# Thresholded attention on one core: first queries loaded and transposed another way, the last two groups' queries picked by one-hot products, and a new step order

## The chip, the cores and the metric

The kernel runs on one core of a Trainium2 chip. A core has five engines with an instruction queue each: TensorE (PE in the profile; its weight loads are PEld), VectorE (DVE), ScalarE (ACT), GpSimd (POOL) and SyncE (SP), which here only issues DMAs. The metric is the device time of one execution in microseconds, the median of several runs.

## What is computed

Eight batches of twelve heads, 512 queries and keys of 64 numbers. Softmax weights at or under the threshold are set to zero, and the rest is normalised again:

```python
batch, heads, seq, dim = 8, 12, 512, 64          # Q, K, V float32, threshold 0.1
scores = np.einsum('bhqd,bhkd->bhqk', Q, K) * scale
weights = np.exp(scores - np.max(scores, axis=-1, keepdims=True))
weights = weights / (np.sum(weights, axis=-1, keepdims=True) + 1e-10)
weights = np.where(weights > threshold, weights, 0)
weights = weights / (np.sum(weights, axis=-1, keepdims=True) + 1e-10)
return np.einsum('bhqk,bhkd->bhqd', weights, V)
```

With random inputs few weights pass the threshold, and most output rows are zero.

## The kernel before

**Cheap pass, over everything.** The 96 heads are 48 pairs (`hp`, two heads each), 24 quads (`hq`) and 12 groups (`j`, eight heads). For every pair the keys and queries are brought to a layout with the 64 numbers on the partitions. Keys: loaded as float32, transposed on PE (`ktr`, line 336), evicted from PSUM (`kev`, to `kt`, float32), cast to float16 by POOL (`kf`). Queries: loaded by quads in runs of 1 KB (`load_q`), cast to float16 (`qmix`, POOL or VectorE), transposed (`qtr`, line 369), evicted (`qev`). Then for each of four chunks of 128 keys one PE step makes the transposed scores of both heads (`qk`, line 379), 128 x 1024 in PSUM, and ACT takes the exponential (`exp`, line 385) or VectorE approximates it through the bits of an integer (line 387): 192 such steps. Products with a matrix `groups` (`d`, line 391; eight steps of four products for a pair) and a maximum (`dred`, line 399) tell for every query whether it may have a weight above the threshold.

**Exact pass, over the rows found.** Once for each group, 32 slots for each of its four pairs: `flags`, `size` (a bound on the norms, from `qsq` and `ksq`), `rank` (a running count on PE), `key`; `oh` compares slot numbers with the ranks and gives one-hot columns (line 428); `idx` multiplies them with row numbers (line 439); `half` and `idxev` make the index; `gather` fetches the found query rows by an indirect DMA of POOL; `split` puts each into the half of its head; `xtr` transposes them (line 467), `xev` evicts; `xqk` makes their exact scores in float32 (line 479); `xexp`, `tv`, `found` (line 496), `vidx`; `fetch` gets the value rows by an indirect DMA into a zeroed tile (`vzero`); `scatter` writes them to the output, which `z` (512 KB zero writes, on SP) has cleared. The names `load_first_q`, `do_first_tr` and `do_first_ev` are the first quad's own path: its queries are loaded as float32 pairs in runs of 256 bytes, half of them by ACT's queue, and transposed as float32 on PE (line 348). `heat`, `warm` and `spare` are products of zeros on PE without a user.

**Order.** Every step is declared with `add(name, {engine: (occupation, latency)}, dependencies, ...)`. The table `ORDER` holds a finished result of a search: the steps in program order, two digits each, and a string of bits that says which engine takes a step that has a choice. Each engine runs its own steps strictly in that order, and waits where a dependency isn't ready. PSUM is three tiles `sc` (128 x 1024) and two tiles `sm` (128 x 512); key loads have six buffers of a pair, query loads four of a quad. In program order the end of the kernel is: last exponentials, `dred` 46 and 47, `flags` to `idxev` of group 11, and the gather, split, products, fetch and scatter of groups 9, 10 and 11.

Of the kernel before, what the change touches and what calls it, by code (L numbers as in the profile page):

```python
# [55 lines left out]
def kernel(  # L56
# [19 lines left out]
    nc = tc.nc  # L76
# [39 lines left out]
    def by_pairs(ap):  # L116
# [16 lines left out]
        "0401020005060D0BN7N0080t0703N2N5N3090L0J0P0A0M0C0K0u0Q0E0NN4N10F0v200G0H0cN60x210s0O0y0z0d0-0g0a0+0R0S0T120U0V1K"  # L133
        "0W100e0X0Y0h0b22110Z240f15261628190i0j0k1A252p3y2n2o0l170m1R270r2B130n0o29181S2A1P141L1N1B1Q1C1D1E1M2T1F0p1G0q2W"
        "2E1H1I1O1T1U1c2s1J2u1d1V1W2X2F1X2r2C1Y1Z2D1a2t2a2I2w1b1e1f2b2v2y1g2J2x2G2U1h1i2-1j2V2H312Y2K301k3x3w4j4i4h1l3-3E"
        "412L332M2N1m2O322Z1n1o2m341p2P2z3H2+2Q2R432S3I443+3F40423G454m35362c3738393A2d3B3C3J4l3K3L4n2e3D3M2f4p2g462h2i2j"
        "6d2l4C48473N4o3O3P5q3Q3R4A2k3S3T4D493U3V4N4s4q4O4U4B4E4F4G4H4I4r581q1r4J4K4L4P4V3X3W1s3Y1y4S4v5s4M6b5r5v4T1t1u3Z"
        "5x5D4Q4w5E5u3a5z4g4R5+5Q4t4u5w5y3b3c4W3d4X4Y5B4Z4z3e4x3f5C5-4+3g8X6c7m4a4b604y6H1v4c3h4d3i4e5F594-50615152536454"
        "5A5G5566625H5I5J5K4f6Z1w6563675L565M5N5O6f9g3j6K6L6g575P6i6h6k68696A6B6C6D6M6I6j5S6E6m6l5R6F5T5U6G6N6J3k5V5W5X3l"
        "6O721x3m5Y6P796n7A5Z6o7l7k8W8VAR233n7p5a7r3o6r6t6p6s5b7K5c6u7t6Q6R6q7o7q7s73771z5d7v7u7L74786S6v6w6T6U6V6x756y6W"  # L140
        "6X6z6+6-7w808T6Y769f4k7x707B710w7C7y7D7E818B8a8c3p5e7F7+7G7H7I7z8e8C7J8Z7-8f8G8b5f8283848D858d6a5g3q8U9e7nAPAQ8H"
        "86875h1+889j7M8g9l898I5i8A8J8E8l7N8F7O9n8y5t7P8j8m8k9o8h8z8i8K7Q8L5j7R9i8-8+7S9k7T8n8MBZBa0ICL909m8N7U938O8P8Q8R"
        "9EAT8oBY7V7W8SAN9F9p9194AV9w8p928q8rAX8s8t8u8v9u8w95967XAU9798999v9A9x9BA5AW9CAC9s8x9q9DAYADAa9G9H9I9tAZ9JA8A69r"
        "5k9KA99y9z9+9L9M7YAsA79-AxAfA05mAg7ZB9AA7aBd5lA1Ay7bA2ABA37cAbAc7gAhAv9NA4AEAiAFAGAH9OAIAdAwBcAtAeBeCJCKDU3zBf9P"
        "9QAuBhAJAzAKBgALCNCPA+Bi9RAOCO7dAMBjCRBmBkBlDTCQB-A-B0B1B2B3B4B5BqAjAkB6AlAmBoAnFOBnAoBrApBpB7CHAqCSArC0C6C2BsC1"
        "BtCTDSEDEFC3CUBA9SCmDXBuDZC7BvBwBxBy9TBz9UB+CVCXCY9VCWCZDWB8D2CpDY9WBBBCCaDaBDC4BECqBFCnCbCIBGDbC5C8CcBHDcEBD33r"
        "9a1-CoDdC9CACBCCEI3sDv9XEKCtDgCdG9FMEECDCECeCfCFCgChDeCuDhCGDfDiBICiCjCkCrBJEHDjBKCsClDkEJEMCvCwELENCxCyCzC+9YC-"
        "D0DlD1BLE0DwEOD4ETDmEgDnE1D5DoD6DxFREUDpD77eD8EREnEjDqESEoEkFNHI6e7fFTBMDrDsD9DtDADuEVEPBND+FVBOEWEzEQDBFWBPD-Dy"
        "FQEhEiFSBQEXEYEZEaG7EbDCDzElGBEcG5DDBRECDEEdFU7h5n3tEeEfG8BSGCGDFXGEFcEm2qGFEpEqGGFYFaHHHGI3FdFpFZErEsGHEtE2E3Eu"
        "FeE4EvEw5o7iFbFfE5E6FqE7E8ExE9FgDFGIBUFrI1JCDVI2FsFwFtFhFiFjFkFlFmEyEAFxGaBTE+FnE-GJHLFuHNFoF0FvF1HPF2GNHKGKHQDG"  # L150
        "GbHMDHGOGtF3DIGPHOGcF4GsF5DJGQFyGfGLFzF+DKF-G0G1G2BV5pHRHjF6GhJAJBJzCMGgG6GMGdHUF7F8GiI6G3GRGSHVG4GTGUGVGeGWHkGX"
        "GYHYHSGjGkHlHTGlGmGZ7jF9DLGnGoGpDMI8GqIAHZI5GrIBGuHoJFJH9ZI7HmGvJJI4HpHnHWGwI9GxGyGzI0H-JKICHqIDHXG+HrIFIEHaHbIU"
        "FAIGJvG-HcHdFBHeHfHgIXJE3uFC9bDNIVJGIYJIHhFDJLIJIWIHHiIZFEIIH0HsHtJdHuIKHvIaHwH1HxBbHyHzJwH2IbJMJiILH+IMINIO9hJD"
        "L6J+JxJyL5IcIPIQJNIRJjK03vFFH3K2ISJQJgJRIdIeIfIgIhIiIjIkJ-ImInLrITJOIlJhIoK1JSIpK4JPIqK3JkJeIrL48YLtJTK5K6JUJlIs"
        "KOJVItJWJXIuJfKPFG9cK9KBJmJnJoJYJZJpJqJaJbKQKCL9H4FILBJrJsLwJtFHKAK7K8L8KVLAJcJuKWLDH5H6LsHJGAL7FPFJLCLEKDKEKTKR"
        "H7KUKFLFLXLyKGLILvKSASLGLxH8LJLHLzKHDOH99dM0MIDPKIKJKKKLKgKhLpKMKXKYKZLKHALMKNLLLNKaKbL+KcLYLZLaLeL-LOLPKdLQKeLR"
# [53 lines left out]
    def load_first_q(hp, other=nc.sync):  # L210
        q_sb = kload.tile([P, R, 2, D], f32, name="k_sb")
        for part in load_pair(q_sb, Qp, hp, other):
            keep(part)
# [550 lines left out]
```

## Time and profile before

| | us |
|---|---|
| median of 3 runs (lowest, highest) | 208.61 (207.15, 209.53) |
| the profiled execution | 208.51 |
| its span, first to last instruction | 206.8 |
| PE, VectorE, ACT, POOL busy in the span | 183.9, 171.0, 163.1, 108.8 |
| first exponential starts | 7.68 |
| last exponential ends | 181.07 |
| last `flags` starts | 185.11 |
| last scatter's instruction ends | 202.55 |

The mean granted TensorE clock was 0.969 of full speed. PE's times are modelled at their ends, so a busy PE isn't PE at its peak. In lines of the profile a row begins with the line of the kernel, the engine and the operation, then output and inputs by name; in lines in order of time it begins with start and duration in us, and what stands in brackets is the engine's idle time before it and what ended that. DMAs moved 38.86 MB in 69,589 packets, 54,356 of them under 512 bytes.

### The profile page before, as it was taken

The numbers are of one execution on the slowest core, as the hardware profiler recorded it, in microseconds if no ns is written. First come the engines' busy times: TensorE is split into PE (matmuls) and PEld (weight loads), VectorE is DVE, ScalarE is ACT, GpSimd is POOL, SyncE is SP. The second block draws the span as 40 slices with busy tenths as digits, with TensorE's granted clock in tenths as the row PEclk, the third lists the DMA queues.
The fourth block names the chain that finished last, engine by engine and source line by source line (L and its number), as shares of the span: only waits on it lengthen the run. The fifth ranks groups of instructions, "written<-read, shape, count | busy, mean of one in ns | idle before, by whom it ended". The sixth has DMA issues, their size and how long they took to land.

```text
span 206.8 us, 7766 instructions
## 1 busy us (share of the span) xinstructions
PE 183.9 (89%) x3235; PEld 122.4 (59%) x3237; DVE 171.0 (83%) x320; ACT 163.1 (79%) x194; POOL 108.8 (53%) x176
## 2 busy tenths in 40 slices
PE   7888999999999999999999988899989999868900
PEld 4554758666756677576677566576657567652200
DVE  6679998999889899989999795989979989642650
ACT  2798998979989999998999988879978899601200
POOL 5025046607467419254656776286665666344661
PEclk9999999999999999999999999999999999696995
DMA  6999799783996599749776279999399500000000
GB/s 138 238 288 258 185 257 269 212 224 89 277 338 190 182 284 275 206 109 251 231 236 149 75 204 241 384 394 210 101 323 412 220 6 8 10 8 4 7 13 11
DMA packets 69589, 38.86 MB, mean 188 GB/s; under 512 B 54356, under 2 KB 66276, under 8 KB 69552
## 3 DMA queue, kind: packets, MB, share of 16 engines
q1 hardware_dynamic: 67344, 37.50, 64.4%
q0 software_dynamic: 1152, 0.59, 1.7%
q8 instruction: 26, 0.43, 0.9%
q10 hardware_dynamic: 1056, 0.26, 0.6%
q14 instruction: 11, 0.09, 0.2%
HBM read 25.95 MB, written 12.98 MB: 188 GB/s over the span
## 4 chain that ended last, share of the span: by engine, by line
PE 65%; DVE 13%; issue 6%; ACT 5%; DMA 4%; POOL 3%; another core or an unknown queue 1%; POOLq 1%; SPq 0%; DVEq 0%; ACTq 0%
PE sc L379 22%; PE sm L391 19%; DVE e L387 6%; PE sc L336 5%; PE sm L479 4%; PE sm L412 4%; PE sm L369 3%; ACT e L385 3%; PE sm L439 3%; DMA k_sb<-in_K_dram 2%; DVE stat L399 2%; DVE qt L321 2%; DMA vsel<-in_V_dram,vidx 1%; PE sc L259 1%; POOL out_dram L193 1%
## 5 line engine op out<-in xcount | busy, mean ns | idle before, releaser
L385 ACT ACTIVATE e<-sc 128x1024 bf16<-128x1024 f32 x140 | 135.8, 1031 | 13.0 <-PE sc L379 11.8
L379 PE MATMUL sc<-qt,kf 64*128 64x512 f16 x384 | 65.2, 384 | 4.5 <-DVE e L387 2.8
L391 PEld LDWEIGHTS <-e 128*128 128x128 bf16 x1536 | 52.5, 99 | 24.4 <-issue 23.8
L387 DVE TENSOR_SCALAR e<-sc 128x1024 int16<-128x1024 f32 x52 | 63.2, 1218 | 4.5 <-PE sc L379 3.2
L391 PE MATMUL sm<-groups,e 128*128 128x64 bf16 x1536 | 62.8, 194 | 2.0 <-issue 1.2
L323 POOL CAST kf<-kt 128x512 f16<-128x512 f32 x46 | 29.7, 660 | 45.1 <-ACT kt L319 34.2
L399 DVE TENSOR_REDUCE stat<-sm 128x8 f32<-128x512 f32 x48 | 32.6, 684 | 9.6 <-PE sm L391 3.0
L379 PEld LDWEIGHTS <-kf 64*128 64x128 f16 x384 | 18.9, 94 | 19.5 <-issue 11.2
L323 POOL CAST qm<-q_sb 128x512 f16<-128x512 f32 x40 | 26.9, 684 | 3.2 <-DMA q_sb<-in_Q_dram 3.1
L193 POOL DMA_INDIRECT qsel<-in_Q_dram,idx x12 | 13.3, 1108 | 18.7 <-DVE idx L448 13.7
L336 PE MATMUL sc<-identity_f,k_sb 64*128 64x64 f32 x368 | 19.3, 226 | 0.7 <-DMA k_sb<-in_K_dram 0.7
L336 PEld LDWEIGHTS sc<-identity_f,k_sb 64*128 64x128 f32 x368 | 16.7, 138 | 3.7 <-DMA k_sb<-in_K_dram 1.0
L319 ACT COPY kt<-sc 128x1024 f32<-128x1024 f32 x16 | 16.2, 1013 | 1.4 <-PE sc L379 0.7
L193 POOL DMA_INDIRECT vsel<-in_V_dram,vidx x12 | 12.9, 1076 | 3.3 <-issue 1.6
L321 DVE COPY qt<-sm 128x1024 f16<-128x1024 f16 x20 | 13.6, 682 | 1.2 <-PE sc L379 1.2
L369 PE MATMUL sm<-identity_h,qm 128*128 128x128 f16 x184 | 14.1, 219 | 0.5 <-DVE stat L399 0.5
L193 POOL DMA_INDIRECT out_dram<-vsel,idx x12 | 12.8, 1064 | 3.2 <-issue 2.9
L479 PE MATMUL sm<-kt,xq 128*32 128x512 f32 x96 | 13.7, 642 | 0.9 <-DVE xq L321 0.6
L359 DVE TENSOR_SCALAR qsq<-qt 128x1024 int16<-128x1024 int16 x24 | 13.3, 560 | 0.0
L369 PEld LDWEIGHTS <-qm 128*128 128x128 f16 x184 | 10.6, 97 | 2.6 <-issue 2.2
L412 PE MATMUL sm<-heads,qsq 128*128 128x2 bf16 x192 | 11.0, 163 | 1.0 <-issue 1.0
L412 PE MATMUL sm<-heads,ksq 128*128 128x2 bf16 x192 | 11.4, 165 | 0.5 <-issue 0.5
(94 smaller groups left out, 168.5 us busy)
## 6 DMA issues: line engine op xcount, KB each, us to landing
out_dram<-zero SPq DMA_DIRECT2D x24, 512.0 KB
k_sb<-in_K_dram SPq DMA_DIRECT2D x95, 128.0 KB
q_sb<-in_Q_dram SPq DMA_DIRECT2D x23, 512.0 KB
k_sb<-in_Q_dram SPq DMA_DIRECT2D x3, 128.0 KB
qsel<-in_Q_dram,idx POOLq DMA_INDIRECT x12, 4.5
vsel<-in_V_dram,vidx POOLq DMA_INDIRECT x12, 3.0
out_dram<-vsel,idx POOLq DMA_INDIRECT x12, 2.2
k_sb<-in_K_dram ACTq DMA_DIRECT2D x1, 128.0 KB
```

What stands on the lines that cost most here:

```text
L193: return keep(nc.gpsimd.indirect_dma_start(**args))
L321: keep(nc.vector.tensor_copy(dst, src))
L323: keep(nc.gpsimd.tensor_copy(dst, src))
L336: keep(nc.tensor.matmul(buffer("sc", ("ktr", hq))[:, at:at + D], lhsT=k_sb[rows, r, :, :].rearrange("p h d -> p (h d)"), rhs=identity_f32[ ...
L369: keep(nc.tensor.matmul(buffer("sm", ("qtr", hq))[:].bitcast(f16)[:, at], lhsT=buffer("qm", hq)[:, at], rhs=identity_h[:], is_transpose=Tr ...
L379: keep(nc.tensor.matmul(buffer("sc", ("qk", hp, c))[:, h * S:(h + 1) * S], lhsT=pair("kf", hq)[ps, n, c * P:(c + 1) * P], rhs=pair("qt", h ...
L385: keep(nc.scalar.activation(e[:], sc[:], ACTF.Exp, scale=scale))
L387: keep(nc.vector.tensor_scalar(e[:].bitcast(i16), sc[:], BITS_A, BITS_B, op0=ALU.mult, op1=ALU.add))
L391: keep(nc.tensor.matmul(buffer("sm", ("d", hp))[:, j * G:(j + 1) * G], lhsT=buffer("e", (hp, c))[:, j * P:(j + 1) * P], rhs=groups[:], sta ...
L399: keep(nc.vector.tensor_reduce(T["stat", j][:, n, :], buffer("sm", ("d", hp))[:].rearrange("p (c g) -> p c g", g=G), axis=AX.X, op=ALU.max))
L412: keep(nc.tensor.matmul(rk[:, at:at + 2], lhsT=sq[:, n % 2, r * P:(r + 1) * P], rhs=heads[:], start=True, stop=True))
L479: keep(nc.tensor.matmul(buffer("sm", ("xs", j))[sl, :], lhsT=xq[:, sl], rhs=pair("kt", 2 * j + n // 2)[:, n % 2], start=True, stop=True, t ...
```

## The change

Four things. The first quad's queries come like all others: quad layout, runs of 1 KB, cast to float16 by `qmix`, and transposed as float16; their first half is one DMA on ACT's queue, ahead of all others. Both halves of the first keys go out on SP. For the last two groups (10 and 11) the one-hot is float32 in another layout, `idx` uses a float32 copy of the row numbers, and a new step `sel` multiplies the queries, which still lie in SBUF, with the one-hot, straight into the layout that `xev` evicts; `gather`, `split` and `xtr` are gone for these groups. `ORDER` is a new search result, with its declared durations changed in places.

```diff
-    load_k(0, nc.scalar)
+    q_sb = qload.tile([P, 4, R, D], f32)
+    T["q", 0] = q_sb
+
+    def load_first_q(n, eng):
+        keep(eng.dma_start(out=q_sb[:, 2 * n:2 * n + 2].rearrange("p h r d -> p h (r d)"), in_=Q4[0][:, 2 * n:2 * n + 2]))
+
     load_first_q(0, nc.scalar)
+    load_k(0)
+    load_first_q(1, nc.sync)
     load_k(1)
-    load_first_q(1)
...
+        keep(nc.vector.tensor_copy(row_f[:], row_no[:]))
...
     def do_first_tr(n, which, eng):
-        tp = buffer(("sm", "sc")[which], ("first", n))
-        src = T.pop((("k", "q32")[which], n))
         for r in range(R):
-            keep(nc.tensor.matmul(tp[:, r * P:(r + 1) * P], lhsT=src[:, r, :, :].rearrange("p h d -> p (h d)"),
-                                  rhs=identity_f32[:], is_transpose=True, start=True, stop=True))
+            at = slice(r * P, (r + 1) * P)
+            if which == 0:
+                keep(nc.tensor.matmul(buffer("sm", ("first", n))[:, at], lhsT=T["k", n][:, r, :, :].rearrange("p h d -> p (h d)"),
+                                      rhs=identity_f32[:], is_transpose=True, start=True, stop=True))
+            else:
+                keep(nc.tensor.matmul(buffer("sc", ("first", n))[:].bitcast(f16)[:, at], lhsT=pair("qm", 0)[:, n, at],
+                                      rhs=identity_h[:], is_transpose=True, start=True, stop=True))
...
     def do_onehot(j, eng):
...
+        if j >= NO - 2:
+            oh = work.tile([P, C2, 4, SLOTS], f32, name="oh_f")
+            keep(nc.vector.tensor_tensor(
+                out=oh[:], in0=slot_no[:, :, 0].unsqueeze(1).unsqueeze(1).to_broadcast([P, C2, 4, SLOTS]),
+                in1=key.rearrange("p n c -> p c n").unsqueeze(3).to_broadcast([P, C2, 4, SLOTS]), op=ALU.is_equal))
...
     def do_idx(j, eng):
...
+            if j >= NO - 2:
+                one, rows = oh.rearrange("p c n s -> p c (n s)")[:, c, :], row_f
...
+    def do_sel(j, eng):
+        oh = T["oh", j]
+        for n in range(4):
+            q_sb = T["q", 2 * j + n // 2]
+            for r in range(R):
+                for h in range(2):
+                    keep(nc.tensor.matmul(buffer("sm", ("xp", j))[h * D:(h + 1) * D, n * SLOTS:(n + 1) * SLOTS],
+                                          lhsT=q_sb[:, 2 * (n % 2) + h, r, :], rhs=oh[:, h * R + r, n, :],
+                                          start=(r == 0), stop=(r == R - 1), tile_position=(0, h * D)))
...
+        if near:
+            stage("sel", {"PE": (0.95, 1.2)}, [("oh", j)] + [("q", hq) for hq in (2 * j, 2 * j + 1)], do_sel, takes=[("sm", ("xp", j))], gives=[("oh", j)])
+        else:
+            stage("gather", {"POOL": (1.45, 6.4, 0.1)}, [("idxev", j)] + ([("split", j - NS)] if j >= NS else []), do_gather)
+            stage("split", {"POOL": (0.4, 0.55), "DVE": (0.21, 0.37)}, [("gather", j), ("half", j)], do_split, takes=[("qb", j)])
+            stage("xtr", {"PE": (0.17, 0.40)}, [("split", j)], do_xtr, takes=[("sm", ("xp", j))], gives=[("qb", j)])
+        stage("xev", {"DVE": (0.2, 0.35), "ACT": (0.2, 0.36)}, [("sel" if near else "xtr", j)], do_xev, gives=[("sm", ("xp", j))], takes=[("xq", j)])
```

What the new order does, by engine. The steps with a choice fall on ACT and VectorE so: exponentials 145 and 47 (140 and 52 before), `kev` 13 and 10 (16 and 7), `xev` 6 and 6 (4 and 8); `qmix` on POOL and VectorE 44 and 4 (40 and 6), now with the first quad's two among them. At the end VectorE has, behind the last exponential: `qsq` 22 and 23, `dred` 46, `dred` 47, `split` 9, `flags` 11, `xev` 9, `key` 11, `oh` 11, `tv` 9, `idxev` 11, `found` 9. PE has the sizes of group 11, `xtr` 9, `rank` 11, `xqk` 9, `idx` 11, `sel` 11, `xqk` 10, `xqk` 11. POOL has `fetch` 8, scatter 4, `gather` 9, scatters 5, 6, 8 and 7, fetches 9, 10 and 11, scatters 9, 10 and 11.

More of the change, by code (lines that the diff above doesn't have):

```diff
@@ L208, in load_q @@
         keep(nc.sync.dma_start(out=q_sb[:].rearrange("p h r d -> p h (r d)"), in_=Q4[hq]))
[L210 to L213, printed above, removed]
-        T["q32", hp] = q_sb
-    load_k(0, nc.scalar)
+    q_sb = qload.tile([P, 4, R, D], f32)
+    T["q", 0] = q_sb
+    def load_first_q(n, eng):
+        keep(eng.dma_start(out=q_sb[:, 2 * n:2 * n + 2].rearrange("p h r d -> p h (r d)"), in_=Q4[0][:, 2 * n:2 * n + 2]))
     load_first_q(0, nc.scalar)
+    load_k(0)
+    load_first_q(1, nc.sync)
     load_k(1)
-    load_first_q(1)
     warm = consts.tile([P, S], bf16)
@@ L271 @@
     row_no = consts.tile([P, C2, 5], f16)
+    row_f = consts.tile([P, C2, 5], f32)
     keep(nc.vector.memset(row_no[:], 0.0))
@@ L644 @@
         stage("vidx", {"POOL": (0.22, 0.36), "DVE": (0.12, 0.28)}, [("found", j)], do_vidx, gives=[("half", j)])
-        stage("vzero", {"POOL": (0.12, 0.25)}, [("gather", j)], do_vzero, takes=[("vsel", j)])
+        stage("vzero", {"POOL": (0.12, 0.25)}, [("idxev" if near else "gather", j)], do_vzero, takes=[("vsel", j)])
         stage("fetch", {"POOL": (1.45, 1.5)}, [("vidx", j), ("vzero", j)], do_fetch)
```

115 lines of the change are left out of this document (59 added, 56 removed).

## The prediction

> **What bounds the kernel now.** I read the page first (busy time, then the chain that ended last), then the table of equal stretches, then the start and the end instruction by instruction.
>
> ```profile
> span 206.8 us, 7766 instructions
> PE 183.9 (89%) x3235; PEld 122.4 (59%) x3237; DVE 171.0 (83%) x320; ACT 163.1 (79%) x194; POOL 108.8 (53%) x176
> ...
> PE 65%; DVE 13%; issue 6%; ACT 5%; DMA 4%; POOL 3%; another core or an unknown queue 1%; POOLq 1%; SPq 0%; DVEq 0%; ACTq 0%
> ```
>
> Three engines are nearly full and the chain hops among them. No single engine is the bound: an edit that takes work from one of them helps only as far as the others have room. The stretches (length, then busy us and instructions of PE, PEld, DVE, ACT, POOL, then the granted clock, the DMA share and GB/s) say where it is not so:
>
> ```profile
> 40.00:60.00 20.00, 19.64 (x362) 12.97 (x358) 18.60 (x34) 18.86 (x24) 9.54 (x15) 1.00 0.73 213
> ...
> 120.00:140.00 20.00, 18.82 (x359) 12.97 (x358) 17.04 (x31) 16.52 (x21) 13.71 (x20) 1.00 1.00 321
> ...
> 180.00:207.00 27.00, 13.98 (x159) 6.36 (x159) 11.08 (x32) 3.35 (x8) 12.36 (x16) 0.82 0.05 8
> ```
>
> From 40 to 60 ACT has 18.86 us of 20, from 120 to 140 only 16.52, with the DMA share at 1.00. From 180 on ACT does 3.35 us in 27: that is the last group's chain of small dependent steps, an eighth of the span in which almost nothing overlaps. This end is where the change can act one for one. VectorE's own sequence at the end (start, us):
>
> ```profile
> 179.85 1.22 DVE L387 TENSOR_SCALAR e<-sc 128x1024 int16<-128x1024 f32 x1
> 180.98 0.27 DVE L448 TENSOR_SCALAR idx<-sm,slot_base,half 128x1 int32<-128x1 f32 x1
> 181.21 0.69 DVE L399 TENSOR_REDUCE stat<-sm 128x8 f32<-128x512 f32 x1
> 181.82 0.42 DVE L359 TENSOR_SCALAR ksq<-kf 128x1024 int16<-128x1024 int16 x1
> 184.38 0.69 DVE L399 TENSOR_REDUCE stat<-sm 128x8 f32<-128x512 f32 x1 [2.15 <-remote]
> 185.11 0.18 DVE L403 TENSOR_SCALAR flags<-stat 128x32 bf16<-128x32 f32 x1
> 185.73 0.26 DVE L424 TENSOR_TENSOR keys<-sm,flags 128x96 bf16<-128x96 f32 x1 [0.43 <-PE sm L420]
> 186.02 0.69 DVE L428 TENSOR_TENSOR oh<-slot_no,keys 128x1024 f16<-128x1024 bf16 x1
> ...
> 192.18 0.29 DVE L461 TENSOR_TENSOR qb<-qsel,half 128x128 f32<-128x128 f32 x1
> ...
> 195.82 0.77 DVE L496 SCALAR_TENSOR_TENSOR junk<-xe,tv,key_no 128x512 bf16<-128x512 f32 x1
> ```
>
> The last exponential ends at 181.07; the reduction after it starts only at 184.38, 2.15 us idle on something the trace cannot name; then flags, keys, one-hot, and a hole of 5.5 us between the one-hot (186.71) and the split of the gathered queries (192.18). The two queues that fill the hole, PE's and POOL's:
>
> ```profile
> 186.77 0.65 PE L439 MATMUL sm<-row_no,oh 128*128 128x5 f16 x8 [0.20 <-DVE oh L428]
> ...
> 188.59 1.94 PE L479 MATMUL sm<-kt,xq 128*32 128x512 f32 x8
> ...
> 193.74 1.07 PE L479 MATMUL sm<-kt,xq 128*32 128x512 f32 x8 [0.26 <-DVE xq L321]
> ```
>
> ```profile
> 188.21 1.08 POOL L193 DMA_INDIRECT qsel<-in_Q_dram,idx  x1 [3.82 <-DVE qb L461]
> ...
> 195.87 1.04 POOL L193 DMA_INDIRECT vsel<-in_V_dram,vidx  x1 [0.30 <-issue]
> 197.62 1.01 POOL L193 DMA_INDIRECT vsel<-in_V_dram,vidx  x1 [0.71 <-issue]
> 198.94 1.02 POOL L193 DMA_INDIRECT out_dram<-vsel,idx  x1 [0.30 <-DMA vsel<-in_V_dram,vidx]
> 200.27 1.00 POOL L193 DMA_INDIRECT out_dram<-vsel,idx  x1 [0.30 <-issue]
> 201.57 0.98 POOL L193 DMA_INDIRECT out_dram<-vsel,idx  x1 [0.30 <-issue]
> ```
>
> The rest is three fetches and three scatters, about 1.3 us apart on POOL, and 4.2 us from the last scatter's end (202.55) to the end of the span.
>
> **The end, from the flags on.** Call the start of the last flags F (185.11). Before, the last group's score product starts at 193.74, F+8.6. The change takes the last two groups' gather, split and transpose away and puts sel in: 32 float32 products of 64 columns by 32. Each float32 product is two records here (four in the code of xqk, eight in its row), so 64. The new order puts xqk 9 ahead of idx 11, sel 11 ahead of xqk 10 and xqk 10 ahead of xqk 11. By rows: rank ends at F+0.6, keys at 0.9. The one-hot is float32 now; between 0.69 (its row) and 1.22 (the 1.216 that VectorE takes to copy as many float32 elements, row below) I take 1.22: ends 2.1. idx 0.65: ends 2.8. xqk 9, 1.07, lies under the one-hot. sel: the nearest row is the float32 transpose, 16 small products in 0.71, 44 ns each:
>
> ```profile
> 10.69 0.71 PE L336 MATMUL sc<-identity_f,k_sb 64*128 64x64 f32 x16
> ```
>
> 64 of them would be 2.8 us. Its products alternate between the two column halves; xqk's, which use four column quarters, show eight 512-column records in 1.07, so a good part overlaps, and at full overlap of two it would be 1.4, at less array time for 32 columns 1.0. I take 2.0, ends 4.9. xqk 10 on PE, 1.07: 5.95. So xqk 11 starts at F+6.0, and the end gets **2.6 shorter** (4.1 with sel 1.0 and the short one-hot, 1.8 with sel 2.8). The Trainium skill says in "TensorE: Matmul & The Clock Gate", section "LDWEIGHTS (loading the stationary operand)", that a weight load takes its columns divided by 1.2 in ns, and the section on fast weight load leaves float32 out of the fast mode; 64 loads of 64 columns one after another would be an estimated 3.4 us, and the forecast by that 205.6. The row of 16 above, which loads 128 float32 columns sixteen times in 0.71 us, doesn't bear the serial rule out.
>
> From xqk 11 on nothing gains: exponential, found (195.82), fetch at 197.62, 3.9 us after xqk 11's start. In the new order fetch 10 waits behind tv 11 on VectorE (vidx 10 stands after it), so fetch 11 follows it by 1.3 at about the same 3.9. Then three scatters as before. Groups 9 and 10 must be out of the way: fetch 9 now comes ahead of both, and POOL has only scatters between it and gather 9.
>
> **The approach to F.** Before: from 181.07 to 185.11, 4.0 us. The new order has behind the last exponential (again VectorE's) two squares (0.42 each), two reductions (0.69 each) and split 9 (0.29), 2.5, with gaps 2.6: **1.4 less**, if the unnamed 2.15 doesn't come back; 0.7 more if it does. It stands once in the span, at one of 48 reductions, with PE's last product of the pair done 2 us earlier; another order puts other instructions there, so I take it as gone. A new wait: split 9 stands ahead of flags 11 on VectorE, so the last chain waits for gather 9 to land. F is then some 183.7; a fetch takes 3.0 us from issue to the scatter that it frees (195.87 to 198.94), so gather 9 must start by 180.4. Its index stands earlier in the new order, ahead of the last squares and six exponentials, and POOL is busy 53% of the span. I cost it at nothing; every us past 180.4 is paid in full.
>
> **The start.**
>
> ```profile
> 0.81 0.65 SPq L197 DMA_DIRECT2D k_sb<-in_K_dram  x1
> 0.81 0.65 ACTq L197 DMA_DIRECT2D k_sb<-in_K_dram  x1
> ...
> 4.47 1.11 PE L348 MATMUL sm<-identity_f,k_sb 128*128 128x128 f32 x4
> ...
> 5.63 0.59 ACT L319 CAST kf<-sm 128x512 f16<-128x512 f32 x1 [2.14 <-PE sm L348]
> 6.62 0.59 ACT L319 CAST qt<-sc 128x512 f16<-128x512 f32 x1 [0.40 <-PE sc L348]
> 7.68 1.02 ACT L385 ACTIVATE e<-sc 128x1024 bf16<-128x1024 f32 x1 [0.48 <-PE sc L379]
> ```
>
> Both key halves now go out on SP one behind the other (0.65 later for the second), the queries on ACT's queue in one transfer. The first transposes come between 4.47 and 5.12. Then 1.15 to the eviction and 0.59 for kf as before; the query path (POOL cast, four float16 transposes, VectorE's eviction) runs beside it, so one eviction of 0.59 and its wait of 0.40 leave ACT's line. ACT puts kt (0.6) there instead, which covers the first product. First exponential between 7.0 and 7.9; **0.3 less** (0.7 less to 0.2 more). The queries' runs are four times as long, which can bring the next loads earlier, up to 1 us more; I leave that for the range.
>
> **The middle.** The new order gives 145 exponentials to ACT and 47 to VectorE (140 and 52), 13 and 10 key evictions (16 and 7), 44 and 4 query casts to POOL and VectorE (40 and 6).
>
> ```profile
> L385 ACT ACTIVATE e<-sc 128x1024 bf16<-128x1024 f32 x140 | 135.8, 1031 | 13.0 <-PE sc L379 11.8 <-DVE tv L491 0.6
> L319 ACT COPY kt<-sc 128x1024 f32<-128x1024 f32 x16 | 16.2, 1013 | 1.4 <-PE sc L379 0.7 <-PE sm L467 0.3 <-POOL qm L323 0.3
> ...
> L387 DVE TENSOR_SCALAR e<-sc 128x1024 int16<-128x1024 f32 x52 | 63.2, 1218 | 4.5 <-PE sc L379 3.2 <-PE sc L336 1.1
> ...
> L323 POOL CAST qm<-q_sb 128x512 f16<-128x512 f32 x40 | 26.9, 684 | 3.2 <-DMA q_sb<-in_Q_dram 3.1
> ...
> L321 DVE COPY kt<-sc 128x1024 f32<-128x1024 f32 x7 | 8.5, 1216 | 1.4 <-PE sc L336 1.4
> ```
>
> ACT: 5 x 1.03 - 3 x 1.01 = +2.1. VectorE: -5 x 1.22 + 3 x 1.22 = -2.4, less two casts. POOL: 4 x 0.68 = +2.7, less two gathers and two splits. PE: sel 10 for one transpose, +2. These cancel to within 1 us per engine, and PE is the fullest, so the sums give nothing: **0**. What the order itself does to idle time I can't read off; its bounds are the two stretches above. One stretch like 120 to 140 costs 18.86 - 16.52 = 2.3 us of ACT; one or two such stretches fewer or more are -4 to +5.
>
> **Sum:** -2.6 - 1.4 - 0.3 + 0 = -4.3. The profiled execution took 208.5 (span 206.8 and 1.7 around it), the median of the three runs is 208.6, so the two can be used as one: **204.2**.
>
> **Rivals.** (1) The end is shorter but PE runs it at half clock, or the unnamed wait returns.
>
> ```profile
> 186.00:188.00 2.00, 1.80 (x13) 0.78 (x11) 1.20 (x4) 0.00 (x0) 0.00 (x0) 0.76 0.00 0
> 188.00:190.00 2.00, 1.89 (x10) 0.39 (x9) 0.42 (x2) 0.27 (x1) 1.49 (x2) 0.50 0.00 0
> 190.00:192.00 2.00, 1.73 (x14) 0.27 (x10) 0.65 (x2) 0.69 (x2) 0.60 (x1) 0.88 0.05 12
> ```
>
> Here the granted clock fell to 0.50, and a score product took 1.94 where the last one took 1.07. The three stretches lack 0.48 + 1.00 + 0.24 = 1.7 us of full clock; the old order spent part of that on waits, in the new one idx, sel and three score products stand close together, so it could cost 1.7 in full: 205.9; with the 2.1 of the wait instead 206.3, with both 208.0. The Trainium skill says in "TensorE: Matmul & The Clock Gate", section "Part 1: The HAM clock gate", that an idle window of about 3.4 us halves the clock; whether the new end has such a window no row of before shows. (2) **Slower:** the new order piles zero writes and indirect DMAs in front of loads. It puts three 512 KB zero writes (8, 11, 1) on SP among the loads of key pairs 28 to 31 and of quads 15 and 16, where the old order had none, and two more ahead of pairs 33 to 35. A load that comes late leaves ACT and VectorE idle as from 120 to 140. Each stretch that it spoils costs 2.3; two eat the whole gain, and four (208.5 - 4.3 + 9.2) give 213.4. Against it: six pair buffers, and the old order had its own pile at 120 to 165. (3) The order is also better in the middle: one or two spoiled stretches fewer, 201.9 or 199.6. (4) The picked queries aren't what sets the end, because POOL's chain of fetches and scatters is: then only the approach and the start pay, 208.5 - 1.7 = 206.8.
>
> **How the numbers follow.** About 1% is what a measurement of this kernel can tell from no change; the faster bound is 206.5, the slower one 210.7. Forecast 0.44; (1) 0.16, half of it still faster; (2) 0.25, of which 0.06 stops within 1%; (3) 0.10; (4) 0.05. Faster 0.44 + 0.08 + 0.10 = 0.62, rounded down to 0.60; same 0.08 + 0.05 + 0.06, with the rounding 0.19; slower 0.21. Range 200.3 (most of (3)) to 211.5 (half of (2)); the forecast's own range is 201.5 to 206.
>
> **What would show it.** Right: xqk 11 within 6 to 7 us of the last flags (8.6 before); no DMA between idx and sel; last exponential at 180.5 to 181.5; flags some 2.6 us behind it; first exponential at 7.0 to 7.9. Wrong: the last exponential past 183 with stretches of ACT below 17 us in 20; split 9 idle on gather 9; sel over 3 us, or score products near 2 us at a clock of 0.5.

## The result and the profile after

| | before | after |
|---|---|---|
| median of 4 runs, us (lowest, highest) | 208.55 (207.15, 209.53) | 218.39 (217.79, 219.16) |
| ratio (95% interval) | | 1.0479 (1.0410 to 1.0549) |
| span of the profiled execution | 206.8 | 217.4 |
| first exponential starts | 7.68 | 8.43 |
| last exponential ends | 181.08 | 187.96 |
| last `flags` starts (F) | 185.11 | 194.92 |

The change is slower by 9.8 us where 4.3 us less was forecast. The span is split here by three events: the start (to the first exponential), the middle (to the end of the last exponential), the approach (to F) and the rest (from F on). They were 7.7, 173.4, 4.0 and 21.7; they are 8.4, 179.5, 7.0 and 22.5. So of 10.6 us the middle took 6.1, the approach 2.9, the rest 0.8 and the start 0.75. Three of the four forecast terms have the wrong sign, and the middle, put at zero, is the largest loss. Some executions of a kernel take a few per cent longer than its others: the ratios leave them out, and the two profiles that fell on one (marked * in the table of runs) aren't used to compare middle, approach and rest.

The head of the page of after, span, busy time and the chain that ended last:

```profile
span 217.4 us, 8040 instructions
PE 195.7 (90%) x3377; PEld 132.7 (61%) x3379; DVE 173.1 (80%) x317; ACT 165.0 (76%) x196; POOL 110.4 (51%) x176
...
PE 69%; DVE 15%; DMA 4%; issue 4%; ACT 3%; SPq 3%; POOL 1%; POOLq 0%; DVEq 0%
```

ACT and VectorE are busy 2 us longer each, PE 12 us, and PE's part of the chain has grown from 65% to 69%. The stretches (length, busy us and instructions of PE, PEld, DVE, ACT, POOL, granted clock, DMA share, GB/s):

```profile
120.00:140.00 20.00, 19.18 (x337) 12.76 (x329) 17.19 (x30) 17.65 (x23) 11.23 (x18) 0.94 0.70 181
140.00:160.00 20.00, 17.94 (x337) 11.88 (x333) 15.83 (x26) 15.62 (x20) 13.12 (x18) 1.00 0.78 243
...
180.00:217.00 37.00, 27.31 (x364) 19.23 (x362) 16.39 (x40) 8.01 (x15) 13.47 (x14) 0.74 0.04 7
```

From 140 to 160 ACT has 15.62 us of 20 and VectorE 15.83: a thin stretch, as 120 to 140 was before. In the last one the clock is 0.74, with PE busy 27 of 37 us. What PE does there, in order of time (start, duration, what it is; in brackets the wait before it):

```profile
184.04 0.39 PE L386 MATMUL sc<-qt,kf 64*128 64x512 f16 x2
184.36 1.95 PE L455 MATMUL sm<-row_f,oh_f 128*128 128x5 f32 x16
186.24 0.39 PE L386 MATMUL sc<-qt,kf 64*128 64x512 f16 x2
186.56 2.67 PE L464 MATMUL sm<-oh_f,q_sb 128*64 128x32 f32 x50
...
189.52 0.96 PE L464 MATMUL sm<-oh_f,q_sb 128*64 128x32 f32 x14 [0.29 <-issue]
190.42 3.59 PE L398 MATMUL sm<-groups,e 128*128 128x64 bf16 x64
...
198.00 1.95 PE L455 MATMUL sm<-row_f,oh_f 128*128 128x5 f32 x16 [0.83 <-DVE tv L518]
199.88 2.67 PE L464 MATMUL sm<-oh_f,q_sb 128*64 128x32 f32 x64
202.48 2.89 PE L506 MATMUL sm<-kt,xq 128*32 128x512 f32 x16
```

The first six rows hold group 10's chain and what it holds up. `idx` 10, now 16 float32 records in 1.95 us where eight float16 ones took 0.65, stands ahead of the last score product, so the split above counts it in the middle. `sel` 10 stands behind that product, 3.6 us in two pieces, and ahead of the last 64 products `d`, which then take 3.59 us at a lowered clock (in e6, below, 32 of them take 1.09): these two make the loss in the approach. VectorE waits for this, in its own sequence:

```profile
182.13 1.98 DVE L437 TENSOR_TENSOR oh_f<-slot_no,keys 128x1024 f32<-128x1024 bf16 x1
...
192.77 0.69 DVE L406 TENSOR_REDUCE stat<-sm 128x8 f32<-128x512 f32 x1 [4.14 <-PE sm L398]
...
194.92 0.17 DVE L410 TENSOR_SCALAR flags<-stat 128x32 bf16<-128x32 f32 x1
195.92 2.02 DVE L437 TENSOR_TENSOR oh_f<-slot_no,keys 128x1024 f32<-128x1024 bf16 x1
```

And ACT, in its sequence:

```profile
186.67 1.03 ACT L392 ACTIVATE e<-sc 128x1024 bf16<-128x1024 f32 x1 [1.28 <-PE sc L386]
```

ACT stands 1.28 us before its last exponential, VectorE 4.14 before a reduction. Behind F the one-hot takes 2.02 (0.69 before), `idx` 1.95 (0.65), `sel` 2.67; `xqk` 10 and 11 stand in one row of 16 records from 202.48, so `xqk` 11, its second half, begins at about 203.9, F+9.0, where it began at F+8.6. The gather's round trip is gone and nothing is won.

### The profile page after: what moved, and what is told of

The parts are those of the page before. It is cut to its first block, busy times and chain, and to the rows that moved or that the text cites. A ratio compares the mean times of both kernels' runs of the same rounds, so it can differ in the third digit from the quotient of the medians.

```text
span 217.4 us, 8040 instructions
## 1 busy us (share of the span) xinstructions
PE 195.7 (90%) x3377; PEld 132.7 (61%) x3379; DVE 173.1 (80%) x317; ACT 165.0 (76%) x196; POOL 110.4 (51%) x176
## 4 chain that ended last, share of the span: by engine, by line
PE 69%; DVE 15%; DMA 4%; issue 4%; ACT 3%; SPq 3%; POOL 1%; POOLq 0%; DVEq 0%
PE sc L386 22%; PE sm L398 19%; PE sc L339 5%; PE sm L376 5%; PE sm L506 5%; DVE e L394 4%; PE sm L419 4%; PE sm L455 3%; PE sm L464 3%; DMA q_sb<-in_Q_dram 3%; DVE stat L406 2%; SPq L197 2%; ACT e L392 2%; DVE kt L324 2%; DMA vsel<-in_V_dram,vidx 1%
## 5 line engine op out<-in xcount | busy, mean ns | idle before, releaser
L392 ACT ACTIVATE e<-sc 128x1024 bf16<-128x1024 f32 x145 | 140.7, 1031 | 18.6 <-PE sc L386 12.4
L398 PEld LDWEIGHTS <-e 128*128 128x128 bf16 x1536 | 54.0, 100 | 26.1 <-issue 25.1
L398 PE MATMUL sm<-groups,e 128*128 128x64 bf16 x1536 | 64.9, 196 | 2.6 <-issue 0.9
L394 DVE TENSOR_SCALAR e<-sc 128x1024 int16<-128x1024 f32 x47 | 57.2, 1219 | 5.0 <-PE sc L386 4.2
L326 POOL CAST qm<-q_sb 128x512 f16<-128x512 f32 x44 | 29.3, 682 | 10.3 <-DMA q_sb<-in_Q_dram 10.2
L193 POOL DMA_INDIRECT qsel<-in_Q_dram,idx x10 | 11.7, 1174 | 15.1 <-DVE idx L475 12.2
L322 ACT COPY kt<-sc 128x1024 f32<-128x1024 f32 x13 | 13.1, 1017 | 0.9 <-PE sc L339 0.8
L512 ACT ACTIVATE xe<-sm 128x512 f32<-128x512 f32 x12 | 7.3, 610 | 8.5 <-PE sm L506 8.2
L366 DVE TENSOR_SCALAR ksq<-kf 128x1024 int16<-128x1024 int16 x24 | 13.6, 570 | 0.0
L324 DVE COPY kt<-sc 128x1024 f32<-128x1024 f32 x10 | 12.2, 1217 | 0.5 <-PE sc L339 0.5
```

The costliest lines, as they stand in the source:

```text
L193: return keep(nc.gpsimd.indirect_dma_start(**args))
L324: keep(nc.vector.tensor_copy(dst, src))
L326: keep(nc.gpsimd.tensor_copy(dst, src))
L366: keep(nc.vector.tensor_scalar(buffer(which + "sq", hq)[:].bitcast(i16), buffer("kf" if which == "k" else "qt", hq)[:].bitcast(i16), 0x7FF ...
L392: keep(nc.scalar.activation(e[:], sc[:], ACTF.Exp, scale=scale))
L394: keep(nc.vector.tensor_scalar(e[:].bitcast(i16), sc[:], BITS_A, BITS_B, op0=ALU.mult, op1=ALU.add))
```

## The experiments

All were timed beside the kernel before on the same chip, and ratios are to it. The chips differ: before took 207.8 us on the chip of e1 to e4 and 199 to 200 on those of the others. Stretches in the table are read from one profiled execution each, in us.

| run | ratio (95%) | first exp | middle | approach | rest |
|---|---|---|---|---|---|
| e1 new order, gathers, old start | 1.0545 (1.0454–1.0635) | 7.9 | 178.4 | 7.6 | 23.2 |
| e2 new start alone | 206.72 us beside 207.83, no interval | 7.2 | 170.9 | 3.8 | 21.9 |
| e3 one-hot products alone | 1.0568 (1.0457–1.0679) | 7.7 | 174.3 | 2.8 | 29.9 |
| e4 after, with gathers | 1.0507 (1.0400–1.0614) | 8.0 | 175.5 | 7.6 | 23.3 |
| e5 old middle, new end | 1.0387 (1.0321–1.0452) | 8.0 | 168.5 | 6.4 | 23.8 |
| e6 new middle, old end | 1.0164 (1.0092–1.0237) | 7.4 | 170.2 | 2.1 | 22.3 |
| e7 `sel` 10 moved back | 1.0458 (1.0384–1.0533) | 8.1 | 170.2 | 3.1 | 26.2 |
| e8 cheap one-hot, 11 only | 1.0022 (0.9977–1.0067) | 9.1 | 164.8 | 2.1 | 21.2 |
| r1* before again | 0.9996 (0.9958–1.0035) | 7.8 | 168.9 | 2.1 | 23.6 |
| r2 after again | 1.0498 (1.0422–1.0574) | 7.9 | 170.0 | 6.6 | 22.3 |
| e9 e8, another tail order | 0.9843 (0.9766–0.9921) | 8.3 | 164.7 | 2.1 | 19.4 |
| e10* after, cheap one-hots | 1.0211 (1.0117–1.0305) | 7.0 | 171.7 | 6.7 | 19.8 |
| e11 after, gather for 10 | 1.0480 (1.0394–1.0565) | 6.9 | 169.1 | 2.2 | 28.9 |
| e12 e11, cheap one-hot | 1.0320 (1.0237–1.0402) | 7.1 | 170.5 | 2.3 | 22.3 |
| e13 e9, old start | 0.9858 (0.9782–0.9934) | 7.6 | 167.0 | 2.1 | 19.4 |
| r3 e9 again | 0.9842 (0.9759–0.9925) | 8.4 | 164.7 | 2.1 | 19.4 |
| e14 e11, `xtr` 10 out of the way | 1.0303 (1.0260–1.0346) | 8.6 | 167.8 | 2.2 | 24.7 |
| e15 e14, cheap one-hot | 1.0095 (1.0052–1.0138) | 8.3 | 169.3 | 2.2 | 19.9 |

### One part alone, or one part undone

```diff
 e1: ORDER of after
-first loads and first transposes of after
+first loads and first transposes of before
-sel 10, sel 11
+gather, split, xtr of groups 10 and 11
```

> The new order with the old start and with gather, split and transpose for groups 10 and 11. Theory A (the loss is a sum: the order's middle +6.1, the start +0.75, sel and what stands around it about +3): the middle stays lost, the rest goes, 208.5 + 6 = 214 to 216. Rival B (the order makes all of it, the 2.9 us ahead of the last flags and the half clock there too; start and sel are neutral or gain): 217 to 219. Rival C (the first exponential's 0.75 us comes back again and again through the loads, the order itself is no worse): 208 to 210.

```diff
 e2: ORDER of before
-load_k(0, nc.scalar); load_first_q as float32 pairs
+load_first_q(0, nc.scalar); load_k(0); load_first_q(1, nc.sync); load_k(1)
+qmix 0 on POOL, qmix 1 on VectorE
```

> The old order and the old end with the new start alone (quad layout, 1 KB runs, float16 transposes, both key halves on one queue). Theory A: first exponential near 8.4 rather than 7.7 and everything behind it as before, 209.0 to 209.6. Rival B: within 0.4 of before, 208.1 to 208.9. Rival C: the late start grows in the middle, 211 or more.

```diff
 e3: ORDER and start of before
-gather, split, xtr of groups 10 and 11
+sel 10, sel 11 at the place of xtr
```

> The old order and the old start with sel for groups 10 and 11 in the place of their gather, split and transpose. Theory A: one-hot 2.0, index 1.95 and sel 2.7 are 6.6 us where one-hot, index, gather and transpose were about 7.2 for group 11, so the last chain is 0.5 shorter to 1 longer, and group 10's 4.7 us of added PE and VectorE time come on top: 209.5 to 211.5. Rival B: sel is neutral or gains, 206 to 208.6. Rival C: no change, 208 to 209.

```diff
 e4: after, its start too
-sel 10, sel 11
+gather, split, xtr of groups 10 and 11
```

> The changed kernel with gather, split and transpose for groups 10 and 11 in place of sel; new order and new start kept. Theory A: without sel 10 ahead of the last products of pairs 46 and 47 the way from the last exponential to the last flags is near 4 us again (6.96 with sel): 215 to 217. Rival B: the time of the changed kernel or more, 217.5 to 220. Rival C: 217 to 219 as well, since the start is the new one.

e3 tells most. The old order with the one-hot products alone is 5.7% slower, against an expected gain, and its rest grew from 21.7 to 29.9 us. The products alone can cost as much as the whole change. The start alone shows no cost: e2's first exponential came earlier and its median was 1.1 us lower, inside the spread of either. e1 and e4 were meant to price the order. By its time e1 (218.6 us) falls to rival B and e4 (216.9) to theory A, but neither for the reason given there: I had put the transpose of group 10's gathered queries where `xev` had stood, ahead of the last `d`, and PE waited there. In e4's queue of PE:

```profile
185.34 0.48 PE L493 MATMUL sm<-identity_f,qb 128*128 128x128 f32 x1 [3.21 <-DVE qb L487]
```

So their approach of 7.6 us holds a wait of my own making, and they don't price the order's end.

### The middle against the end

```diff
 e5: new start; ORDER of before up to chunk 2 of the exponentials of pair 45
+from there on ORDER of after, with sel 10 and sel 11
```

> The new start, the old order up to the exponential of pair 45, chunk 2, and from there the changed kernel's order with sel for groups 10 and 11. Theory A (order: about +5 in the middle, between 100 and 165 us; sel and its place: about +3 between last exponential and last flags and +1 behind them): first to last exponential 171 to 174, the way to the last flags 6 to 7.5, the rest 22 to 23, in all 209 to 212. Rival B (the loss is the end's, whatever stands ahead of it): 215 or more. Rival C (the loss is the middle's alone): 206 to 208.

```diff
 e6: new start; ORDER of after up to the same point
+from there on ORDER of before, with gathers
```

> The new start and the changed kernel's order up to the same step, from there the old order, with gathers for all groups. Theory A: the middle stays at 176 to 179, the way to the last flags is 4 again and the rest 22, in all 211 to 214. Rival B: 206 to 208. Rival C: 215 to 218.

```diff
 e7: after
-PE: ... sel 10, d 46, d 47, ..., rank 11 ...
+PE: ... d 46, d 47, ..., rank 11, sel 10 ...
-ACT: xev 10 ahead of rank 11
+ACT: xev 10 behind sel 10
```

> The changed kernel, with sel 10 moved from ahead of the last products of pairs 46 and 47 to behind the rank of group 11, where PE waits for the last one-hot, and its eviction with it. Theory A: the way from the last exponential to the last flags falls from 7.0 to about 4, behind the flags sel 10 costs 0 to 1.5 through the exact products of group 9 and the index of group 11: 215 to 217.5. Rival D (the products of pairs 46 and 47 are late because of the clock or the last exponentials, not because of sel 10): 218 to 220.

```diff
 e8: ORDER of before with a new tail, new start; sel for group 11 alone, gather for 10
+oh_f = work.tile([P, C2, 4 * SLOTS], f32, name="oh_f")
+for h, e in enumerate(("ACT", "DVE")):
+    copy(e, oh_f[:, h * R:(h + 1) * R], oh.rearrange("p n s c -> p c (n s)")[:, h * R:(h + 1) * R])
-idx with oh_f and row_f
+idx with oh and row_no, float16
```

> The old order and the new start; sel for group 11 alone, with the one-hot and the index in float16 as before, and a float32 copy of the one-hot made by ACT and VectorE, a half each; transposes and picked queries of groups 10 and 11 in the score tiles, and group 9's exact products ahead of the last index. Theory A (sel's gain was lost to the float32 one-hot at 2.0, the float32 index at 1.95 and to sel 10, not to sel itself): last index 0.65, sel 2.7, last exact products within 6.5 us of the last flags, 2 us less than with the gather: 204 to 205.5. Rival E (sel is no better than the gather even so): 206.5 to 208.5.

The new end costs 3.9% on the old middle, the new middle 1.6% under the old end; together 5.5%, against 5.0% for the whole change on such a chip (r2, below). The end is the larger part: e5 lies past theory A, in rival B's range, and e6 in theory A's. In e7 a later place on PE doesn't hide `sel` 10: the approach is 3.1 where r2 has 6.6, and the rest 26.2 where r2 has 22.3. Its ratio lies at the edge of rival D's times, yet with `sel` 10 out of their way the products were no longer late. e8 takes the two costs away that the trace of after shows: group 10 goes back to a gather, which has time enough there, and group 11's one-hot is written as float16 in 0.69 us as before and only then copied to float32, by halves on two engines, while `idx` stays float16. Against e5, which has the same middle, that wins back 3.7%, and e8 is level with before. A gain was expected, and rival E had none; but in e8's trace the scatter of group 8 stands between POOL's fetches, and PE waits 1.2 us for the split of group 9.

### Again, and the better tail

```diff
 r1: before; r2: after, as they are
```

> The kernel before, unchanged, profiled on the same chip as the three runs beside it. In the first call of runs PE's semaphores came up to 2 us late at a few places of every trace (before: 117.1 to 118.6, 125.6 to 128.9, 136.4 to 138.7 and 181.2 to 184.4), in the second call at none, and the kernel before took 207.8 there and 199.3 here. Theory F (the two chips differ, the kernels don't): a chip with such pauses gives 207 to 209 with the unnamed wait of 2.1 at the last reduction, one without them 198.5 to 200.5 and no such wait. Rival G (the pauses come with the profile and not with the chip): the time and the pauses don't go together.

> The changed kernel, unchanged, on the same chip as the kernel before. Theory F: on a chip without pauses the middle loses only some 2 us (5.5 with them), and the end, with sel, the rest: ratio 1.04 to 1.05, last flags to end 22 to 24, last exponential to last flags 6 to 7. Rival G: ratio 1.045 to 1.055 with the middle at +5.

```diff
 e9: e8
-POOL: split 9; fetch 9, fetch 10, scatter 8, fetch 11
+VectorE: split 9 behind flags 11
+POOL: scatter 8, fetch 9, fetch 10, fetch 11
-PE: xtr 9, rank 11, ...
+PE: rank 11, xtr 9, xqk 9, idx 11, xtr 10, sel 11, xqk 10, xqk 11
```

> The run with the cheap one-hot for group 11 (old order, new start), with GpSimd's order mended: scatter 8 ahead of the fetches rather than between fetch 10 and fetch 11, and the split of group 9 on VectorE with its transpose behind the last rank. Theory A (there GpSimd's scatter, 1.3 us, and the wait for the split, 0.6, ate what sel gained): last flags to the end 19 to 20 (21.2 there, 21.7 before), ratio 0.980 to 0.992. Rival E (sel is no better than the gather): ratio 0.995 to 1.005.

```diff
 e10: after
-float32 one-hot and float32 idx of groups 10 and 11
+the cheap one-hot and float16 idx of e8
```

> The changed kernel with the one-hot and index of groups 10 and 11 in float16 and a float32 copy of the one-hot by ACT and VectorE, a half each; its order is kept. Theory A: sel 11 starts some 2.2 us earlier behind the last flags (2.0 + 1.95 become 0.69 + about 1.1), last flags to the end 20 to 21, ratio 0.009 to 0.013 below that of the changed kernel. Rival H (the end is set by GpSimd's fetches and scatters or by the clock): no more than 0.004 below.

r2 repeats the loss, 1.0498, on a chip on which before takes 199.5 us. So what is peculiar to the chip of the first runs (the last section) isn't the cause. e9, with both mended, beats both kernels: 196.49 us against 199.54. Its PE behind the last flags (175.15):

```profile
177.43 0.67 PE L450 MATMUL sm<-row_no,oh 128*128 128x5 f16 x8
...
178.19 2.06 PE L459 MATMUL sc<-oh_f,q_sb 128*64 128x32 f32 x64
180.18 1.92 PE L501 MATMUL sm<-kt,xq 128*32 128x512 f32 x16
```

`xqk` 11, the second half of the last row, begins at about 181.1, F+6.0: the chain that was forecast, with `idx` 0.67 and `sel` 2.06. What makes it so, in VectorE's sequence:

```profile
176.06 0.69 DVE L435 TENSOR_TENSOR oh<-slot_no,keys 128x1024 f16<-128x1024 bf16 x1
176.78 0.65 DVE L323 CAST oh_f<-oh 128x512 f32<-128x512 f16 x1
```

And in ACT's:

```profile
176.78 1.18 ACT L321 CAST oh_f<-oh 128x512 f32<-128x512 f16 x1 [0.41 <-DVE oh L435]
```

`idx` needs the first row alone; the two copies run beside it. No run gave the kernel with gathers e9's order of scatters; but from the start of `xqk` 11 to the end before takes 13.1 us and e9 13.4, so what e9 gains lies ahead of `xqk` 11, in the chain that `sel` shortens. e10, the cheap one-hot in after and nothing else, won 2.9%, twice and more of what was expected; the expectation had counted group 11's chain alone, and group 10 has one too.

### Taking after apart

```diff
 e11: after, sel and float32 one-hot for group 11 alone
-sel 10
+gather 10 behind gather 9; split 10 on POOL; xtr 10 behind rank 11; xev 10 ahead of oh 11
```

> The changed kernel with sel for group 11 alone; group 10 gets its gather, split and transpose back, the transpose behind the last rank. Theory J (about 6 of the 10 us stand in PE's queue: the float32 one-hot, index and sel of group 10 ahead of the last scores and of the products of pairs 46 and 47): the last exponential 2 earlier, the way to the last flags 2 to 3 rather than 6.5, the rest 21.5 to 23, ratio 1.015 to 1.025. Rival K (the middle's order makes most of it): ratio 1.035 or more.

```diff
 e12: e11
-float32 one-hot and idx of group 11
+the cheap ones of e8
```

> The same with the cheap one-hot for group 11. Theory J: another 2.5 us less behind the last flags, ratio 1.002 to 1.012; what is left above the run with the old order and the same one-hot is the price of the new order, some 2 %. Rival K: 1.025 or more.

```diff
 e13: e9
-new start
+start of before
```

> The old order with the old start and with sel and the cheap one-hot for group 11 alone, so that only the end differs from the kernel before. Theory A: last flags to the end 19 to 20 rather than 21.7, ratio 0.985 to 0.992. Rival L (the gain of that version was the new start's): 0.995 or more.

```diff
 r3: e9, as it is
```

> The same with the new start (run once before, 0.9843), on the same chip as the old start. Theory A: 0.980 to 0.990, and 0.003 to 0.006 below the old start. Rival L: 0.010 or more below it.

e11 got the approach back (6.6 in r2, 2.2 here), and lost 6.6 us behind F. PE's queue there, and the stretch with its clock:

```profile
181.41 0.48 PE L495 MATMUL sm<-identity_f,qb 128*128 128x128 f32 x1 [2.56 <-POOL qb L489]
...
184.51 3.42 PE L456 MATMUL sm<-row_f,oh_f 128*128 128x5 f32 x16
187.85 3.63 PE L465 MATMUL sm<-oh_f,q_sb 128*64 128x32 f32 x64
191.41 3.64 PE L507 MATMUL sm<-kt,xq 128*32 128x512 f32 x16
```

```profile
178.00:196.00 18.00, 15.44 (x134) 9.23 (x132) 5.11 (x16) 2.76 (x9) 5.45 (x8) 0.53 0.02 5
```

PE stands 2.56 us for a split that I had queued on POOL, and the whole chain runs at a clock of 0.53: `sel`, 2.06 in e9, takes 3.63 here, `idx` 3.42. The clock had halved at 178.7, ahead of that wait, and stayed so to 195.7. So the run tells what half clock costs, not what the gather brings. e12 keeps the wait (2.08 us) and stands at 1.0320, where theory J had 1.012 at most. e13 and r3 differ by 0.0016 with intervals of 0.008 each, so the old start and the new can't be told apart, and r3 repeats e9.

```diff
 e14: e11
-split 10 on POOL; xtr 10 behind rank 11; xev 10 ahead of oh 11
+split 10 on VectorE behind oh 11; xtr 10 ahead of sel 11; xev 10 behind sel 11
```

> The changed kernel with sel for group 11 alone and a gather for group 10, as two runs ago, but with the split of group 10 on VectorE behind the last one-hot and its transpose behind the last index, so that PE doesn't stand waiting for the gather and doesn't fall to half clock for it. Theory J (the float32 chain of group 10 in PE's queue costs some 6 us, and the run two calls ago gave that back by a wait of 2.6 us on PE and a half clock of 17 us): last exponential near 176, 2.2 from there to the last flags, 22 to 23 from there to the end, ratio 1.010 to 1.022. Rival K (the rest of the new order makes most of it): 1.035 or more.

```diff
 e15: e14
-float32 one-hot and idx of group 11
+the cheap ones of e8
```

> The same with the cheap one-hot for group 11: last flags to the end 19.5 to 20.5, ratio 0.998 to 1.008 by theory J, so that what the new order costs against the old one with the same end (0.984) is 1.5 to 2.3 %, some 3 to 4.5 us in the middle. Rival K: 1.02 or more.

With the wait out of the way e14 stands at 1.0303, between theory J (1.022 at most) and rival K (1.035): `idx` ran at full clock, `sel` and `xqk` again did not.

```profile
181.68 1.95 PE L456 MATMUL sm<-row_f,oh_f 128*128 128x5 f32 x16 [0.86 <-DVE oh_f L438]
184.24 3.63 PE L465 MATMUL sm<-oh_f,q_sb 128*64 128x32 f32 x64 [0.45 <-DVE idx L476]
187.80 3.53 PE L507 MATMUL sm<-kt,xq 128*32 128x512 f32 x16
```

e15 stands at 1.0095, just past theory J. In it both run at full clock:

```profile
183.78 2.06 PE L459 MATMUL sm<-oh_f,q_sb 128*64 128x32 f32 x64
185.77 1.92 PE L501 MATMUL sm<-kt,xq 128*32 128x512 f32 x16
```

Now the steps lie in one row: r2 1.0498, group 10 back to a gather 1.0303 (e14), the cheap one-hot for group 11 1.0095 (e15), the old order with e9's tail 0.9842 (r3). At 199.5 us that is 3.9 us, 4.1 us and 5.0 us, known to 1.7, 1.2 and 1.9 us by the intervals. The first step crosses chips, and the last changes the order of the middle and of the tail together.

## Why the prediction was wrong

**The end, from the flags on (−2.6; measured +0.8).** The mechanism was right. No DMA lies between `idx` and the products, "I take 2.0" for `sel` was 2.06 at full clock, and in e9, where only group 11 goes this way, `xqk` 11 begins at the F+6.0 that was worked out, the rest is 19.4 us where before had 21.7, and the kernel is 1.6% faster than before. What failed is the price of what `sel` needs. "The one-hot is float32 now; between 0.69 and 1.22 I take 1.22": it took 2.02. "idx 0.65" was carried over from float16: as float32 it took 1.95. Together 2.1 us too little, and the cheap one-hot, which takes both back, is worth 4.1 us from e14 to e15, since the clock then holds too. The other 0.9 us between F+6.0 and F+9.0 came in `sel` (2.67) and `xqk` 10 (half of 2.89), part of them at a clock of 0.50. I had priced the comparison by a copy of as many float32 elements; why it takes 2.02 no run separates. And I had counted for `sel` that a float32 product is two records, but not for `idx`. The estimate of 3.4 us for `sel` by the Trainium skill's rule in "TensorE: Matmul & The Clock Gate", section "LDWEIGHTS (loading the stationary operand)", isn't what full clock shows: 64 records of 64 columns took 2.06 us, 32 ns each.

**The approach (−1.4; measured +2.9).** This is the step with the worst gap in it. I worked out group 11's chain and took group 10's as a transpose replaced: "PE: sel 10 for one transpose, +2" stands under the middle, as a sum per engine. But its one-hot, `idx` and `sel`, some 2.0 + 1.95 + 3.5 us, stand in program order among the last scores and ahead of the last `d`, where each engine takes what comes next, and there it lies on the path: to take it out was worth 3.9 us (r2 to e14). e11, e14 and e15, without it, have an approach of 2.2 us; r2 has 6.6. The new order shows that place before any run, so this could have been seen. The other half of the step held: the unnamed 2.15 us wait doesn't come back in the approach, and `split` 9 ahead of `flags` cost nothing (F came 2.2 us behind the last exponential in e14, with 2.6 forecast). But the 1.4 us of gain hung on that wait, and it belongs to the chip (last section): on the others the old order's end has an approach of 2.1 us (e6), and there was nothing to gain.

**The middle (0; measured +6.1 on the first chip, 3 to 5 in r2 against e13 and e9).** "These cancel to within 1 us per engine, and PE is the fullest, so the sums give nothing" is the third failure. Its own figures don't cancel for any engine: +2.1 on ACT, -2.4 on VectorE and +2 on PE cancel only when summed across engines. Between e15 and r3 the order costs 5.0 us, and 0.8 to 4.6 of it lie in the middle (167.8 and 169.3 in e14 and e15; 164.7 in r3 and 167.0 in e13, with the old order); e6 has 1.6% with an end like before's. In after and r2 `idx` 10, ahead of the last score, lengthens the middle as well. ACT's exponentials between 10 and 172 us, grouped by line, with the idle time before them and what ended it, first of after:

```profile
L392 ACT ACTIVATE e<-sc 128x1024 bf16<-128x1024 f32 x133 | 129.0, 1031 | 14.6 <-PE sc L386 8.5 <-PE sm L398 2.8 <-PE sc L339 2.0
```

The same group of r2:

```profile
L392 ACT ACTIVATE e<-sc 128x1024 bf16<-128x1024 f32 x140 | 135.2, 1033 | 7.7 <-PE sc L386 6.0 <-ACT e L392 0.3
```

And of e9:

```profile
L391 ACT ACTIVATE e<-sc 128x1024 bf16<-128x1024 f32 x139 | 134.3, 1033 | 5.9 <-PE sc L385 5.2
```

On these two chips the new order leaves ACT 1.8 us more idle (after, on its own chip, far more; but e13, with the old order, has 8.4 in all), and at 172 us it has given VectorE 45 exponentials to e9's 51, so five fewer are done in all. ACT is busy 153 to 155 of those 162 us in either, so it has little room for the +2.1 us that the new split gives it. How much of the loss is that and how much the sequence wasn't separated, and the cause in the middle stays open; no run changed only who takes which exponential. Rival (2) had the sign and, with "four stretches", half the size (213.4), but not the mechanism as far as these rows show it: none of ACT's idle time in these rows ends on a DMA. The longest wait for a load in after, 7.7 us for queries, is POOL's, and PE's products waited 0.5 us in all for what POOL makes of them.

**The start (−0.3; measured +0.75).** One profile can't tell. With the same start code the first exponential came anywhere from 6.9 to 9.1 us in the fifteen profiles that have it, in nine of them later than the 7.9 that the forecast allowed, and from 7.6 to 7.9 in the five with the old one. So the forecast of an earlier first exponential failed as often as not. In the whole time, by r3 against e13, the new start is 0.3 us faster, which no interval separates from nothing.

**Rival (1), the clock,** was real and too small. It was priced at 1.7 us; half clock on `sel`, `idx` and `d` cost 1.2 to 1.6 us each where it fell. In after `sel` 10, `d`, `sel` 11 and the last `xqk` row together took an estimated 4.6 us more than such rows at full clock (2.06 for a `sel`, twice 1.09 for `d`, 1.92 for `xqk`).

## What to carry to other kernels

When a change alters the type of a tile, price every instruction that reads or writes the tile again, on all engines: float32 cost this one-hot a factor of three in its comparison and three in its first product, and a late copy of a cheap float16 tile was the better way. A trick that shortens the last dependent chain paid here only in the last chain; for the group before it, the gather ran behind other work, and the products stood in the way of the very work that the last chain waits for. In an order written out by hand, each added instruction costs at its place in its engine's queue, not in that engine's sum.

## What the runs showed of the hardware

**Half clock, and what came ahead of it.** In these traces the granted clock is full or half, and half comes in stretches of 3.4 us or a multiple of it (6.8 from 176.7 in r2, 17.1 from 178.7 in e11), but for the last, which the end of the trace cuts. Two steps of after, cut where the clock changes (columns as above):

```profile
184.00:187.41 3.41, 3.41 (x53) 2.90 (x50) 1.83 (x5) 2.13 (x3) 2.80 (x3) 1.00 0.03 8
187.41:190.82 3.41, 2.99 (x50) 2.74 (x47) 1.21 (x3) 0.56 (x2) 1.74 (x5) 0.50 0.05 12
```

And two of e15:

```profile
180.98:184.39 3.41, 2.51 (x39) 1.41 (x32) 2.46 (x7) 2.05 (x5) 2.56 (x5) 1.00 0.04 11
184.39:187.80 3.41, 3.41 (x67) 1.87 (x64) 0.37 (x3) 0.95 (x3) 1.05 (x1) 1.00 0.06 10
```

In after PE is busy throughout the first step and gets half clock in the next; in e15 it is idle for a quarter of the first and keeps full clock. The step of after holds the float32 `idx` 10. Every step that holds a float32 `idx` at full clock is followed by half clock, eleven of eleven (two each in after, r2, e3, e5 and e7, one in e14), and `sel`, which comes next, pays for it. That it is `idx` and nothing beside it no run shows alone, since the cheap one-hot changed both. Half clock also came without it, behind steps in which PE had stood for 0.4 to 2.2 us (e6 from 172.3, e1 from 187.2), but not behind all such: in e8 PE stood for 1.1 us in the step from 176.2 and kept full clock. The Trainium skill speaks in "TensorE: Matmul & The Clock Gate", section "Part 1: The HAM clock gate", of an idle window of about 3.4 us; here a window in which the profile shows PE busy throughout came ahead of half clock. What counts as idle these runs don't settle. e8, e9, r3 and e15 have no half clock from the last exponentials to the end of the last scores.

**A chip on which PE's signal comes late.** In after, `d` ended at 115.27 and the reduction that needs it began at 117.06, with VectorE idle; in e7, the same steps on another chip, the reduction follows 0.25 us behind. VectorE of after:

```profile
114.38 1.22 DVE L394 TENSOR_SCALAR e<-sc 128x1024 int16<-128x1024 f32 x1 [0.18 <-PE sc L386]
...
117.06 0.69 DVE L406 TENSOR_REDUCE stat<-sm 128x8 f32<-128x512 f32 x1 [1.46 <-PE sc L386]
```

PE of after, the products `d`:

```profile
114.88 0.39 PE L398 MATMUL sm<-groups,e 128*128 128x64 bf16 x8
```

PE of e7:

```profile
113.57 0.39 PE L399 MATMUL sm<-groups,e 128*128 128x64 bf16 x8
```

And VectorE of e7:

```profile
114.21 0.68 DVE L407 TENSOR_REDUCE stat<-sm 128x8 f32<-128x512 f32 x1
```

The unnamed 2.15 us wait of the prediction was of this kind: it stands in the first profile of before, and e6, with the same end on another chip, has an approach of 2.1 us in place of 4.0. Three to five such places are in each profile of before, after and e1 to e4, none in the later ones, and before takes 207.8 us on the chip of e1 to e4 and 199 to 200 on the later ones. What makes the signal late stays open.
